# One step for both head parities in the attention scores of a network's last two layers

## The chip, the cores and the metric

The program runs on one core of one Trainium2 chip. The metric is the device time of one execution in microseconds (us); the median of three runs of the kernel before is 1946.26 us (1945.66 to 1946.44).

## The reference, cut to what matters

Four layers work on 256 tokens of 1024 channels, in float32: one with a recurrent mixer (HGRN2), one with latent attention, and two of a second block, each with feed-forward parts. The change touches only the two attentions in the mixer of the second block's two layers. Both have 8 heads of 64 channels:

```python
# stick-breaking attention
z = jnp.einsum('bhqd,bhkd->bhqk', qi, k).astype(jnp.float32) * scale
past = kpos[None, :] < qpos[:, None]
log_keep = jnp.where(past, jax.nn.log_sigmoid(-z), 0.0)
suffix = lax.cumsum(log_keep, axis=3, reverse=True) - log_keep
w = jnp.where(past, jnp.exp(jax.nn.log_sigmoid(z) + suffix), 0.0)
return jnp.einsum('bhqk,bhkd->bhqd', w.astype(v.dtype), v)
...
# block attention: with 256 tokens a query sees only its own block
s_own = jnp.einsum('bhqd,bhkd->bhqk', qi, k_own).astype(jnp.float32) * scale
s_own = jnp.where(own_pos[None, :] <= qpos[:, None], s_own, -jnp.inf)
p = jax.nn.softmax(jnp.concatenate([s_sel, s_own], axis=-1), axis=-1).astype(v.dtype)
```

## The kernel before

The tokens are two blocks of 128, called 0 and 1 here (`t` in the code); block 1 attends to the keys of both. Weights stream in chunks of 1024 columns per partition; each is split once, on ScalarE (high part, `wh`) and VectorE (low part, `wl`), and both token blocks use it. A projection multiplies the 128 tokens with a chunk by six products of 128x512 columns (three for each of two blocks of rows: L438, L439, L440, by `mm3`). Such a piece is called a chunk step below. Up to 11 split chunks are kept.

The program's work is cut into steps that begin with products on TensorE (`add`). They stand in lanes; a planner (`run`) picks the next step of all lanes by its own clock, from the costs that each step states, its dependences, the free PSUM banks and the free pages of two arenas (`fa` for float32, `ra` for float32r). So each engine's instructions have one fixed order, and a step whose costs change can move everything behind it. Where a step's turn comes, its ScalarE and VectorE instructions are queued there too, and the chunk splits take their places between them.

The mixer (`mixer`, one for each layer and token block) has, beside its projections, these steps:
- `turn` (L1441): four transposes that bring the queries or keys of four pairs of heads to [channel, token]. The two heads of a pair (even and odd parity) lie on rows 0 to 63 and 64 to 127. Queries and keys of the block attention are first rotated on GpSimd.
- `sb_z(g, kb)` (L1462, L1464): stick-breaking scores of the four heads of parity g against key block kb, into one bank: for the diagonal block a product of the identity with the mask (128x512), then four products with 64 rows. Then a chain of ScalarE (absolute value, exponential, logarithm, copy) and VectorE. `sb_suffix` (L1488 and following) and `sb_mix` (L1515) use it.
- `mb_s(i)` (L1547, L1551, L1552): scores of the block attention, 2 units for token block 0 with four heads each and 4 units for block 1 with two heads each, each of one parity in one bank. For every head a mask product of 128 columns and the head's product follow each other; for block 1 the products with the keys of block 0 come ahead. Then `softmax`: maximum on VectorE, exponentials on ScalarE, reciprocal and scaling on VectorE.
- `mb_t` (L1566): four transposes of a unit's weights, copied back by VectorE; `mb_o` (L1587): products with the values.

A float32 product of the program is two records in the trace.

Of the kernel before, what the change touches and what calls it, by code (L numbers as in the profile page):

```python
# [26 lines left out]
# Weights stream through the chip in chunks of at most 1024 columns per partition,  # L27
# loaded two (or so) at a time; each chunk is split once into float32r parts
# (high + low) that both token blocks use.
RAW = 3           # loads in flight  # L30
RING = 11         # split chunks kept
AHEAD = 2         # chunks split ahead of their first use
FAR = 5           # the same, while the engines that split have less than SLACK to do
SLACK = 0.9       # microseconds
LEAD = 6          # chunks token block 0 may be ahead of token block 1
DVE_LEVELS = 3    # levels of HGRN2 whose queries are decayed by the vector engine
SPARE = 3328      # words that a projection of HGRN2 leaves to the heads at work
HOP = 0.4         # from one engine to another, microseconds
ARENA_F = 9728    # float32 words per partition
ARENA_R = 6144    # float32r words per partition  # L40
# [3 lines left out]
class Arena:  # L44
    def __init__(self, tile_, words):
        self.t = tile_
        self.n = words // PAGE
        self.free_at = [0] * self.n     # 0: never used; None: held
        self.clock = 1

    def fits(self, words, spare=0):
        """Room for this many words in all, in pieces of up to 1024."""
        k = (words + PAGE - 1) // PAGE
        if sum(f is not None for f in self.free_at) < k + spare // PAGE:
            return False
        size, want = min(k, 8), max(k // 8, 1)
        run = found = 0
        for f in self.free_at:
            run = 0 if f is None else run + 1
            if run and run == size:  # L60
                found, run = found + 1, 0
        return k == 0 or found >= want
# [29 lines left out]
class Step:  # L92
    """Work that begins with products: its time on the tensor engine, the steps and the chunk that it
    waits for, the PSUM banks that it takes and gives back, and the words (float32, float32r, float32
    to be left free) without which it isn't begun."""
# [14 lines left out]
def constants():  # L110
    """Tables that depend on shapes alone."""
    i = np.arange(P)
    ident = np.eye(P)
    causal = np.where(i[None, :] > i[:, None], NEG, 0.0)       # [query, key]
    strict = np.where(i[:, None] >= i[None, :], NEG, 0.0)      # [key, query]
    after = (i[:, None] > i[None, :]).astype(float)            # [key', key]
    ones = np.ones((P, P))
    parts = {"ident": ident, "causal": causal, "strict": strict, "after": after, "ones": ones}
    # decay exponents of HGRN2: for a level of half-length m the pair (s, t) meets at
    # the middle of the 2m-block that splits them  # L120
# [29 lines left out]
def network_kernel(ctx: ExitStack, tc: tile.TileContext, A, out):  # L150
    nc = tc.nc
    mm = nc.tensor.matmul
    # the clock by which steps are ordered: when each engine is free, and how far the
    # work behind the step at hand has come
# [8 lines left out]
    def mark():  # L163
        """The banks of the step are read."""
        chain[2] = chain[0]

    class Engine:
        """An engine whose instructions are charged by the columns they write."""
# [24 lines left out]
    def act(o, i, func, with_ln=False, **k):  # L193
        """An activation; with_ln: natural logarithms come with it."""
# [36 lines left out]
    rope1 = sb.tile([P, 2, 2, 32], F32, name="rope1")      # [token, block, cos|sin, :]  # L231
    rope2 = sb.tile([P, 2, 2, 8], F32, name="rope2")
    krT = sb.tile([P, 2, 2 * P], F32, name="krT")     # rows of the other head of a pair are zero
# [20 lines left out]
    chunks, loads = [], []  # L254

    def load(dmas, views):
        """dmas: (columns of the raw buffer as a function, source); views: chunks cut from it."""
# [11 lines left out]
    def load_cols(w, k0, c0, n):  # L269
        """Four blocks of rows, n columns of each: two chunks of 2 x n."""  # L270
# [4 lines left out]
    def load_pair(w, c0, wc, n):  # L275
        """Two blocks of rows, wc columns: chunks of 2 x n."""
# [4 lines left out]
    def load_rows(w, k0):  # L281
        """Two whole blocks of rows: two chunks of 1 x 1024."""
# [4 lines left out]
    def load_gu(wg, wu, j, half):  # L287
        """Columns of gate and up side by side."""
        v = lambda r: r.rearrange("p (k g f) -> p k g f", k=4, g=2)
        dmas = []  # L290
        size = 4 if loads else 2     # the first chunk is waited for
# [20 lines left out]
    def with_gain(chs, g):  # L312
        """The rows of the chunks, which follow each other, are scaled by the gains from column g of gcol."""
# [29 lines left out]
    def splits(now, upto, slack=None):  # L343
        """Split chunks up to the given one; with a slack, only while the engines are idle enough."""
# [16 lines left out]
    def add(t, key, pe, emit, deps=(), chunk=None, banks=(), acq=(), rel=(), lane="", need=(0, 0)):  # L361
        """Steps of one lane run in order; the main lane of a token block is called ""."""
# [4 lines left out]
    def ready(s):  # L367
        if not fa.fits(s.need[0], *s.need[2:]) or not ra.fits(s.need[1]):
            return None
# [78 lines left out]
    def project(t, key, chs, xh, xl, evac, deps=(), n=512, behind=None, need=512, spare=0):  # L448
        """out[tokens, n] over the blocks of rows of chs, evacuated by evac(psum); behind: adds steps
        that follow the first chunk."""  # L450
# [21 lines left out]
    def down(t, key, chs, lhs, deps, first, evac=None, end=None):  # L472
        """Blocks of rows of a product with 1024 columns, summed in two banks: the first half of the
        columns of all, then the second. The last step has an evac(bank, half)."""
# [16 lines left out]
    def downs(t, key, chs, lhs, deps, evac, end=None):  # L491
        """The blocks one by one, but the last two together."""
# [5 lines left out]
    def transposes(t, key, g, deps):  # L498
        """X -> X^T in parts (XH, XL), scaled by the gains from column g of gcol per row, if given."""
# [25 lines left out]
    def split_scaled(src, g, h, l):  # L525
        """Parts of src * g, one gain per partition and block, src in PSUM."""
# [18 lines left out]
    pending = [None, None]     # statistics, put behind the first chunk that follows  # L545

    def norm_tr(t, key, g, xdep):
        """RMS statistics of X and its transposed parts scaled by the gain g."""
# [104 lines left out]
    def ple(t, li, W, g, xdep):  # L653
# [31 lines left out]
        for n in (0, 1):  # L685
            def evac(o, n=n):
                s = F(512)
                c = slice(n * 512, n * 512 + 512)
                # sigmoid(y) = (1 + tanh(y / 2)) / 2, the last half in pw
# [25 lines left out]
    def hgrn_tables(t):  # L715
        """Bounds of the forget gates, decay exponents and masks."""
        for hf in (0, 1):
            hg["lb", hf] = F(D)     # the bound, and 1 - the bound
# [43 lines left out]
    def hgrn(t, W, g, xdep):  # L762
# [12 lines left out]
        def evac(hf, c):  # L775
            def f(o):
# [24 lines left out]
                else:  # L801
                    s = F(512)
                    # sigmoid(y) = (1 + tanh(y / 2)) / 2
# [20 lines left out]
        def diagonal(hf):  # L824
            """A token's own key: sum of q * k."""
# [12 lines left out]
        def suffix(hf):  # L838
            """Keys decayed to the end of the block, token-major."""
# [30 lines left out]
        def stepA(hd):  # L870
            """Keys and queries decayed to the middle of the blocks of every level."""
# [45 lines left out]
        def stepB(hd):  # L917
            """Scores as [key, query]: what the halves of a block of 32 and more give goes straight
            to its place, the four small levels are computed for their later tokens and masked."""
# [112 lines left out]
    kvs = {}  # L1032

    def rope1_table(t):
        """cos and sin of position * inverse frequency, reduced to [-pi, pi]."""
# [829 lines left out]
```

## Time and profile before

| | |
|---|---|
| runs | 1945.66, 1946.26, 1946.44 us |
| profiled execution, span | 1944.4 us |
| TensorE matmul busy | 1915.5 us (99%) |
| VectorE, ScalarE, GpSimd busy | 1208.8 us (62%), 1026.6 us (53%), 181.5 us (9%) |
| first and last start of L1464 | 1187.5 and 1596.4 us |
| first and last start of L1552 | 1245.6 and 1656.5 us |

The span is the profiled execution's own, from its first to its last instruction; its time as a run was not recorded, and the span is 1.9 us below the median of the runs. TensorE is busy nearly all the time, in the two mixers (near 1170 to 1290 us and 1535 to 1660 us) too, so its queue is what to read first; an idle time of another engine costs nothing by itself.

### The profile page before, as it was taken

To read this page: it belongs to the slowest core of one execution; us is meant where nothing else is said; L and a number is where in the kernel's file an instruction comes from. 1 tells how busy PE (TensorE), PEld (TensorE's weight loads), DVE (VectorE), ACT (ScalarE), POOL (GpSimd) and SP (SyncE) were. 2 spreads that over 40 slices of the span, in tenths; PEclk is the share of its full clock that TensorE was granted. 3 is DMA by queue.
4 is the path that set the end of the run, shared out by engine and by line. 5 is a ranking of instruction groups with operands and counts; after the bars stand their busy time and mean duration, and the time that the engine had idled before them with its cause. 6 is when DMAs were issued, how large, how long until landed. Compare 5 with 4: busy or idle time off the path is not lost. (4 is left out here: it accounts for less than half of the span.)

```text
span 1944.4 us, 25096 instructions
## 1 busy us (share of the span) xinstructions
PE 1915.5 (99%) x9484; PEld 1586.2 (82%) x9484; DVE 1208.8 (62%) x1804; ACT 1026.6 (53%) x1596; POOL 181.5 (9%) x320
## 2 busy tenths in 40 slices
PE   8999989999999999999999999999999999999998
PEld 6888878888888888899888888778888887888886
DVE  6567769855567555556655566666655665666554
ACT  6565655644457555665544456544544465544442
POOL 1021334200001000232000000200000002000000
PEclk9999999999999999999999999999999999999999
DMA  9656313666546655333666653345656534556661
GB/s 289 223 183 192 117 60 107 195 196 200 182 149 194 208 183 189 109 114 132 194 194 187 201 173 131 124 165 189 206 184 214 175 109 131 176 192 196 193 215 45
DMA packets 215509, 331.30 MB, mean 170 GB/s; under 512 B 8462, under 2 KB 150236, under 8 KB 215388
## 3 DMA queue, kind: packets, MB, share of 16 engines
q1 hardware_dynamic: 215020, 329.14, 52.3%
q8 instruction: 74, 1.21, 0.3%
q10 hardware_dynamic: 368, 0.56, 0.1%
q14 instruction: 47, 0.39, 0.1%
HBM read 328.62 MB, written 1.05 MB: 170 GB/s over the span
## 5 line engine op out<-in xcount | busy, mean ns | idle before, releaser
L181 DVE TENSOR_TENSOR wl<-raw,wh 128x1024 fp32r<-128x1024 f32 (+1 forms) x520 | 631.7, 1229 | 424.7 <-ACT wh L204 423.6
L204 ACT ACTIVATE wh<-raw 128x1024 fp32r<-128x1024 f32 (+1 forms) x520 | 538.3, 1050 | 345.2 <-PE bank L440 312.9
L438 PE MATMUL bank<-wh,xh 128*128 128x512 f32 x1696 | 682.2, 402 | 2.5 <-ACT wh L204 2.5
L440 PE MATMUL bank<-wh,xl 128*128 128x512 f32 x1696 | 664.6, 392 | 0.0
L439 PE MATMUL bank<-wl,xh 128*128 128x512 f32 x1696 | 663.6, 391 | 1.0 <-DVE wl L181 1.0
L440 PEld LDWEIGHTS bank<-wh,xl 128*128 128x128 f32 x1696 | 320.1, 189 | 68.7 <-DVE xl L181 0.8
L438 PEld LDWEIGHTS bank<-wh,xh 128*128 128x128 f32 x1696 | 320.6, 189 | 65.1 <-ACT wh L204 3.3
L439 PEld LDWEIGHTS bank<-wl,xh 128*128 128x128 f32 x1696 | 321.1, 189 | 62.9 <-DVE wl L181 3.3
L438 PE MATMUL bank<-wh,ra 128*128 128x512 f32 (+1 forms) x736 | 286.3, 389 | 0.5 <-ACT ra L204 0.5
L440 PE MATMUL bank<-wh,ra 128*128 128x512 f32 (+1 forms) x736 | 283.5, 385 | 0.1
L439 PE MATMUL bank<-wl,ra 128*128 128x512 f32 (+1 forms) x736 | 283.1, 385 | 0.0
L204 ACT ACTIVATE fa<-bank,stat 128x256 f32<-128x256 f32 (+4 forms) x198 | 95.8, 490 | 184.2 <-PE bank L440 132.8
L204 ACT ACTIVATE fa<-bank 128x512 f32<-128x512 f32 (+3 forms) x228 | 102.4, 480 | 141.7 <-PE bank L440 87.5
L440 PEld LDWEIGHTS bank<-wh,ra 128*128 128x128 f32 x736 | 138.1, 188 | 27.4 <-DVE ra L181 1.1
L438 PEld LDWEIGHTS bank<-wh,ra 128*128 128x128 f32 x736 | 138.4, 188 | 26.3 <-ACT ra L204 0.7
L439 PEld LDWEIGHTS bank<-wl,ra 128*128 128x128 f32 x736 | 138.3, 188 | 25.7
L181 DVE SCALAR_TENSOR_TENSOR wl<-raw,gcol,wh 128x512 fp32r<-128x512 f32 (+1 forms) x192 | 136.3, 759 | 35.5 <-ACT wh L204 33.6
L181 POOL TENSOR_TENSOR stat<-stat,mhalf 128x1 f32<-128x1 f32 (+1 forms) x34 | 28.1, 826 | 1306.3 <-DVE stat L181 1306.3
L204 ACT ACTIVATE wh<-raw,gcol 128x512 fp32r<-128x512 f32 (+1 forms) x192 | 126.2, 709 | 29.3 <-PE bank L440 21.1
L181 POOL TENSOR_TENSOR fa<-fa 128x64 f32<-128x64 f32 (+4 forms) x156 | 98.3, 654 | 178.5 <-DVE fa L181 102.0
L204 ACT ACTIVATE ra<-bank 128x256 fp32r<-128x256 f32 (+1 forms) x158 | 61.9, 391 | 83.4 <-PE bank L590 43.4
L181 DVE SCALAR_TENSOR_TENSOR fa<-bank,stat,fa 128x256 f32<-128x256 f32 x88 | 42.5, 483 | 84.6 <-ACT fa L204 84.6
(160 smaller groups left out, 1296.0 us busy)
## 6 DMA issues: line engine op xcount, KB each, us to landing
raw<-in_ffn_w_in_dram SPq DMA_DIRECT2D x174, 512.0 KB, 4.9
raw<-in_ffn_w_out_dram SPq DMA_DIRECT2D x44, 1024.0 KB, 4.9
raw<-in_w_in_dram SPq DMA_DIRECT2D x40, 1024.0 KB, 5.1
raw<-in_w_ffn_gate_dram SPq DMA_DIRECT2D x44, 512.0 KB, 4.0
raw<-in_w_ffn_up_dram SPq DMA_DIRECT2D x44, 512.0 KB, 5.0
raw<-in_w_ffn_down_dram SPq DMA_DIRECT2D x22, 1024.0 KB, 4.9
raw<-in_a_w_in_dram SPq DMA_DIRECT2D x16, 1024.0 KB, 5.4
raw<-in_ple_w_gate_dram SPq DMA_DIRECT2D x8, 1024.0 KB, 5.0
```

Source lines behind the costliest of these rows:

```text
L181: return f(o, *a, **k)
L204: nc.scalar.activation(o, i, func, **k)
L438: mm(o, xh, ch.h[:, kk, cols], start=start, stop=False)
L439: mm(o, xh, ch.l[:, kk, cols], start=False, stop=False)
L440: mm(o, xl, ch.h[:, kk, cols], start=False, stop=stop)
```

## The change

`sb_z` and `mb_s` now make both parities in one step, with two banks. The masks come first, one product per bank (identity times a 128x512 mask, or two heads' 128x256 in token block 1), then the heads' products, where even and odd parity, so rows 0 to 63 and 64 to 127 of the array, take turns, each into its own bank. In `sb_z` the three ScalarE instructions of both parities stand ahead of the VectorE part, and one buffer `sp` serves both parities in turn. `mb_t` writes the transposed weights back into its source. The steps' stated costs and arena needs change with it, and `fits` looks for the float32r room in pieces of 512 words.

```diff
@@ Arena.fits, ready @@
-    def fits(self, words, spare=0):
+    def fits(self, words, spare=0, piece=8):
...
-        size, want = min(k, 8), max(k // 8, 1)
+        size, want = min(k, piece), max(k // piece, 1)
...
-        if not fa.fits(s.need[0], *s.need[2:]) or not ra.fits(s.need[1]):
+        if not fa.fits(s.need[0], *s.need[2:]) or not ra.fits(s.need[1], 0, 4):
@@ mixer: stick-breaking scores @@
-        def sb_z(g, kb):
-            name = K(f"z{g}{kb}")
+        def sb_z(kb):
+            name = K(f"z{kb}")
+            banks = [f"{name}.{g}" for g in (0, 1)]
             def emit():
-                b = B(name)
+                bs = [B(n) for n in banks]
                 qT, kT = four(sh["qsT", t]), four(sh["ksT", kb])
-                r = slice(64 * g, 64 * g + 64)
                 if kb == t:
-                    mm(b, identb, strict.rearrange("p a b -> p (a b)"), start=True, stop=False)
+                    for b in bs:
+                        mm(b, identb, strict.rearrange("p a b -> p (a b)"), start=True, stop=False)
                 for i in range(4):
-                    mm(b[:, i * P:(i + 1) * P], kT[r, i], qT[r, i], start=kb != t, stop=kb != t or i == 3)
-                u, sp = F(512), F(512)
-                h, l = R(512), R(512)
-                act(u.ap, b, AF.Abs)
-                act(u.ap, u.ap, AF.Exp, with_ln=True, scale=-1.0)
-                act(u.ap, u.ap, AF.Ln, with_ln=True, bias=one)
-                stt(sp.ap, b, 0.0, u.ap, op0=OP.max, op1=OP.add)
-                act(h.ap, sp.ap, AF.Copy)
-                tt(u.ap, b, sp.ap, op=OP.subtract)
-                mark()
-                tt(l.ap, sp.ap, f32(h.ap), op=OP.subtract)
+                    for g, b in enumerate(bs):
+                        r = slice(64 * g, 64 * g + 64)
+                        mm(b[:, i * P:(i + 1) * P], kT[r, i], qT[r, i], start=kb != t, stop=kb != t or i == 3)
+                us = [F(512), F(512)]
+                sp = F(512)
+                for b, u in zip(bs, us):
+                    act(u.ap, b, AF.Abs)
+                    act(u.ap, u.ap, AF.Exp, with_ln=True, scale=-1.0)
+                    act(u.ap, u.ap, AF.Ln, with_ln=True, bias=one)
+                for g, (b, u) in enumerate(zip(bs, us)):
+                    h, l = R(512), R(512)
+                    stt(sp.ap, b, 0.0, u.ap, op0=OP.max, op1=OP.add)
+                    act(h.ap, sp.ap, AF.Copy)
+                    tt(u.ap, b, sp.ap, op=OP.subtract)
+                    if g:
+                        mark()
+                    tt(l.ap, sp.ap, f32(h.ap), op=OP.subtract)
+                    st["u", g, kb], st["sp", g, kb] = u, (h, l)
                 sp.free()
...
-            add(t, name, 0.86 + 0.22 * (kb == t), emit,
+            add(t, name, 0.9 + 0.44 * (kb == t), emit,
...
-                lane="z", need=(1024, 1024))
+                lane="z", need=(1536, 2048))
@@ mixer: block attention @@
-        def mb_s(i):
+        def mb_s(w):
...
-                if t == 1:
-                    kT = four(sh["kmT", 0])
-                    for j, pr in enumerate(prs):
-                        mm(b[:, j, :P], qT[r, pr], kT[r, pr], start=True, stop=True)
-                kT = four(sh["kmT", t])
-                for j, pr in enumerate(prs):
-                    o = b[:, j, t * P:]
-                    mm(o, identb, causal[:, 0], start=True, stop=False)
-                    mm(o, qT[r, pr], kT[r, pr], start=False, stop=True)
-                p = F(512)
-                softmax(b, nh, p.ap.rearrange("p (h s) -> p h s", h=nh))
+                for b in bs:
+                    mm(b[:, :, t * P:], identb, causal[:, :nh], start=True, stop=False)
+                for kb in range(nk):
+                    kT = four(sh["kmT", kb])
+                    for j, pr in enumerate(mb_pairs(w)):
+                        for hf, b in enumerate(bs):
+                            r = slice(64 * hf, 64 * hf + 64)
+                            mm(b[:, j, kb * P:(kb + 1) * P], qT[r, pr], kT[r, pr], start=False,
+                               stop=kb == nk - 1 and j == nh - 1)
+                for hf, b in enumerate(bs):
+                    p = st["P", 2 * w + hf] = F(512)
+                    softmax(b, nh, p.ap.rearrange("p (h s) -> p h s", h=nh))
...
-            add(t, name, 1.0, emit, deps=[K("tqm")] + [f"{kb}.{key}.tkm" for kb in range(nk)],
-                banks=[name], lane="s", need=(512, 0))
+            add(t, name, 1.2, emit, deps=[K("tqm")] + [f"{kb}.{key}.tkm" for kb in range(nk)],
+                banks=banks, lane="s", need=(1024, 0))
@@ mb_t: the transposed weights go back over p @@
-                p.free()
-                y = F(512)
-                vec.tensor_copy(y.ap, b)
-                st["PT", i] = y
+                vec.tensor_copy(p.ap, b)
+                st["PT", i] = p
```

The change moves instructions, on TensorE inside the steps and on all engines by the planner. On TensorE, the scores of token block 0 in the first mixer (`ident` is the identity, `strict` the mask, `fa` queries and keys); before:

```order
L1462 LDWEIGHTS identb
L1462 MATMUL bank_111<-strict,identb 128x512
L1464 MATMUL bank_111<-fa 128x128 x4
L1462 LDWEIGHTS identb
L1462 MATMUL bank_112<-strict,identb 128x512
L1464 MATMUL bank_112<-fa 128x128 x4
```

and now:

```order
L1465 LDWEIGHTS identb
L1465 MATMUL bank_111<-strict,identb 128x512
L1465 LDWEIGHTS identb
L1465 MATMUL bank_112<-strict,identb 128x512
L1469 MATMUL bank_111<-fa 128x128
L1469 MATMUL bank_112<-fa 128x128
L1469 MATMUL bank_111<-fa 128x128
L1469 MATMUL bank_112<-fa 128x128
L1469 MATMUL bank_111<-fa 128x128
L1469 MATMUL bank_112<-fa 128x128
L1469 MATMUL bank_111<-fa 128x128
L1469 MATMUL bank_112<-fa 128x128
```

The two masks stand together, and the products change bank, so row half, from one to the next.

On ScalarE, from the evacuation of the projected block attention keys of token block 0 (the first row) to the copy of their transposes (the last row); between them GpSimd rotates these keys. Before, with the transposed queries of block 1 and two splits (`wh`) between:

```order
L204 ACTIVATE fa<-bank_107 128x512
L204 ACTIVATE fa<-bank_109 128x512
L204 ACTIVATE wh_75<-raw_65 128x1024
L204 ACTIVATE wh_76<-raw_65 128x1024
L204 ACTIVATE fa<-bank_108 128x512
```

and now, where the keys of block 1 and the mix of block 1 (`ra`) are between as well:

```order
L204 ACTIVATE fa<-bank_107 128x512
L204 ACTIVATE fa<-bank_114 128x512
L204 ACTIVATE fa<-bank_113 128x512
L204 ACTIVATE wh_75<-raw_65 128x1024
L204 ACTIVATE ra<-bank_112 128x512
L204 ACTIVATE wh_76<-raw_65 128x1024
L204 ACTIVATE fa<-bank_110 128x512
```

On TensorE the transposes of these keys stood behind four transposes and two chunk steps; they now stand behind five chunk steps, four transposes and the 16 products of a mix.

On ScalarE, around the exponentials of block 1's four softmax units (rows with `fa,stat<-bank`); before, from the copy of block 0's output (`ra`):

```order
L204 ACTIVATE ra<-bank_112 128x512
L204 ACTIVATE fa,stat<-bank_111,stat 128x256 x2
L204 ACTIVATE fa,stat<-bank_113,stat 128x256 x2
L204 ACTIVATE fa,stat<-bank_107,stat 128x256 x2
L204 ACTIVATE fa,stat<-bank_108,stat 128x256 x2
L198 ACT_TABLE_LOAD
L204 ACTIVATE fa<-bank_110 128x512
```

and now, after the splits `wh_67` and `wh_68`:

```order
L204 ACTIVATE wh_67<-raw_63 128x1024
L204 ACTIVATE wh_68<-raw_64 128x1024
L204 ACTIVATE fa,stat<-bank_112,stat 128x256 x2
L204 ACTIVATE fa,stat<-bank_110,stat 128x256 x2
L204 ACTIVATE wh_69<-raw_64 128x1024
L204 ACTIVATE fa,stat<-bank_114,stat 128x256 x2
L204 ACTIVATE fa,stat<-bank_109,stat 128x256 x2
L204 ACTIVATE wh_70<-raw_65 128x1024
```

All four units were one run; now two of a step stand together, with a split between the steps, and the split `wh_70`, which the first chunk step of the next weight waits for, stands behind all four.

## Rows read from the trace of the kernel before

**Rows 1.** The page, part 1: busy us, share of the span, instructions.
```profile
PE 1915.5 (99%) x9484; PEld 1586.2 (82%) x9484; DVE 1208.8 (62%) x1804; ACT 1026.6 (53%) x1596; POOL 181.5 (9%) x320
```

**Rows 2.** Windows: busy us by engine (instructions), then granted clock, DMA share, GB/s.
```profile
1267.90:1274.80 6.90, 6.90 (x24) 5.21 (x25) 3.62 (x10) 2.91 (x12) 0.00 (x0) 0.51 0.12 46
1633.20:1640.00 6.80, 6.80 (x17) 5.11 (x18) 4.00 (x13) 4.38 (x16) 0.00 (x0) 0.50 0.00 0
```

**Rows 3.** Timeline of TensorE, first mixer, block 0's z steps: start, us, engine, line.
```profile
1187.14 0.39 PE L1462 MATMUL bank<-strict,identb 128*128 128x512 bf16 x1
1187.46 1.16 PE L1464 MATMUL bank<-fa 64*128 64x128 f32 x8
1188.54 0.39 PE L1462 MATMUL bank<-strict,identb 128*128 128x512 bf16 x1
...
1189.95 0.50 PE L438 MATMUL bank<-wh,xh 128*128 128x512 f32 x1
```

**Rows 4.** The same, block 1's z steps.
```profile
1208.07 0.39 PE L1462 MATMUL bank<-strict,identb 128*128 128x512 bf16 x1
1208.39 2.05 PE L1464 MATMUL bank<-fa 64*128 64x128 f32 x16
...
1212.67 0.50 PE L438 MATMUL bank<-wh,xh 128*128 128x512 f32 x1
```

**Rows 5.** The same, keys' transposes and block 0's softmax scores; [idle before, releaser].
```profile
1241.34 0.39 PE L439 MATMUL bank<-wl,xh 128*128 128x512 f32 x1
1241.56 0.39 PE L440 MATMUL bank<-wh,xl 128*128 128x512 f32 x1
1243.61 0.66 PE L1441 MATMUL bank<-ident,fa 128*128 128x128 f32 x4 [1.66 <-POOL fa L181]
...
1245.49 0.23 PE L1551 MATMUL bank<-causal,identb 128*128 128x128 bf16 x1
...
1250.10 0.50 PE L438 MATMUL bank<-wh,xh 128*128 128x512 f32 x1
```

**Rows 6.** The same, block 1's softmax scores.
```profile
1263.66 0.71 PE L1547 MATMUL bank<-fa 64*128 64x128 f32 x4
...
1265.04 0.37 PE L1552 MATMUL bank<-fa 64*128 64x128 f32 x1
1265.05 0.37 PE L1547 MATMUL bank<-fa 64*128 64x128 f32 x1
...
1270.76 0.79 PE L438 MATMUL bank<-wh,xh 128*128 128x512 f32 x1
```

**Rows 7.** The same, second mixer.
```profile
1627.61 0.66 PE L1441 MATMUL bank<-ident,fa 128*128 128x128 f32 x4 [1.66 <-POOL fa L181]
...
1629.49 0.23 PE L1551 MATMUL bank<-causal,identb 128*128 128x128 bf16 x1
...
1634.74 0.79 PE L438 MATMUL bank<-wh,xh 128*128 128x512 f32 x1
...
1650.75 0.71 PE L1547 MATMUL bank<-fa 64*128 64x128 f32 x4
...
1656.69 0.50 PE L438 MATMUL bank<-wh,xh 128*128 128x512 f32 x1
```

**Rows 8.** Timeline of VectorE, first mixer, softmax units, split and copy.
```profile
1247.90 0.69 DVE L181 TENSOR_REDUCE stat<-bank 128x4 f32<-128x512 f32 x1 [0.79 <-PE bank L1552]
...
1251.23 0.68 DVE L181 TENSOR_REDUCE stat<-bank 128x4 f32<-128x512 f32 x1
...
1254.64 1.22 DVE L181 TENSOR_TENSOR wl<-raw,wh 128x1024 fp32r<-128x1024 f32 x1
1255.78 0.68 DVE L181 COPY fa<-bank 128x512 f32<-128x512 f32 x1
...
1265.57 0.69 DVE L181 TENSOR_REDUCE stat<-bank 128x2 f32<-128x512 f32 x1 [0.47 <-PE bank L1552]
...
1268.07 0.68 DVE L181 TENSOR_REDUCE stat<-bank 128x2 f32<-128x512 f32 x1
```

More of the change, by code (lines that the diff above doesn't have):

```diff
@@ L1475, in emit @@
+                for g, (b, u) in enumerate(zip(bs, us)):
[7 more added lines that the diff above has]
+                    st["u", g, kb], st["sp", g, kb] = u, (h, l)
                 sp.free()
-                st["u", g, kb], st["sp", g, kb] = u, (h, l)
@@ L1477, in sb_z @@
-            add(t, name, 0.86 + 0.22 * (kb == t), emit,
-                deps=[K("tqs"), f"{kb}.{key}.tks"], banks=[name],
-                lane="z", need=(1024, 1024))
+            add(t, name, 0.9 + 0.44 * (kb == t), emit,
+                deps=[K("tqs"), f"{kb}.{key}.tks"], banks=banks,
+                lane="z", need=(1536, 2048))
         def sb_suffix(g, kb):
@@ L1501, in emit @@
                 act(u.ap, u.ap, AF.Exp)
-            add(t, name, 0.43 if kb == t else 0.86, emit, deps=[K(f"z{g}{t}"), K(f"z{g}{kb}")],
+            add(t, name, 0.43 if kb == t else 0.86, emit, deps=[K(f"z{t}"), K(f"z{kb}")],
                 banks=[name], lane="y")
@@ L1530, in mixer, with mb_pairs @@
         nh = 4 if t == 0 else 2
-        def mb_heads(i):
-            return [nh * (i // 2) + j for j in range(nh)], i % 2
-        def mb_s(i):
-            name = K(f"s{i}")
+        def mb_pairs(w):
+            return [nh * w + j for j in range(nh)]
+        def mb_s(w):
+            name = K(f"s{w}")
+            banks = [f"{name}.{hf}" for hf in (0, 1)]
             def emit():
-                b = B(name).rearrange("p (h s) -> p h s", h=nh)
+                bs = [B(n).rearrange("p (h s) -> p h s", h=nh) for n in banks]
                 qT = four(sh["qmT", t])
-                prs, hf = mb_heads(i)
-                r = slice(64 * hf, 64 * hf + 64)
-                if t == 1:
-                    kT = four(sh["kmT", 0])
-                    for j, pr in enumerate(prs):
-                        mm(b[:, j, :P], qT[r, pr], kT[r, pr], start=True, stop=True)
-                kT = four(sh["kmT", t])
-                for j, pr in enumerate(prs):
-                    o = b[:, j, t * P:]
-                    mm(o, identb, causal[:, 0], start=True, stop=False)
-                    mm(o, qT[r, pr], kT[r, pr], start=False, stop=True)
-                p = F(512)
-                softmax(b, nh, p.ap.rearrange("p (h s) -> p h s", h=nh))
-                st["P", i] = p
-            add(t, name, 1.0, emit, deps=[K("tqm")] + [f"{kb}.{key}.tkm" for kb in range(nk)],
-                banks=[name], lane="s", need=(512, 0))
+                for b in bs:
[12 more added lines that the diff above has]
+                banks=banks, lane="s", need=(1024, 0))
         def mb_t(i):
@@ L1566, in emit @@
                     nc.tensor.transpose(b[:, j * P:(j + 1) * P], p.ap[:, j * P:(j + 1) * P], ident)
-                p.free()
-                y = F(512)
-                vec.tensor_copy(y.ap, b)
-                st["PT", i] = y
-            add(t, name, 0.44, emit, deps=[K(f"s{i}")], banks=[name],
-                lane="x", need=(512, 0))
+                vec.tensor_copy(p.ap, b)
+                st["PT", i] = p
+            add(t, name, 0.44, emit, deps=[K(f"s{i // 2}")], banks=[name], lane="x")
         def mb_o(w):
@@ L1579, in emit @@
                 ys = [st.pop(("PT", 2 * w + hf)) for hf in (0, 1)]
-                prs, _ = mb_heads(2 * w)
-                for j, pr in enumerate(prs):
+                for j, pr in enumerate(mb_pairs(w)):
                     for hf in (0, 1):
@@ L1606, in mixer @@
             turn(n)
+        for kb in reversed(range(nk)):
+            sb_z(kb)
         for g in (0, 1):
-            for kb in reversed(range(nk)):
-                sb_z(g, kb)
             for kb in reversed(range(nk)):
@@ L1614, in mixer @@
             turn(n)
-        for i in range(2 * nk):
-            mb_s(i)
-            mb_t(i)
-            if i % 2:
-                mb_o(i // 2)
+        for w in range(nk):
+            mb_s(w)
+            mb_t(2 * w)
+            mb_t(2 * w + 1)
+            mb_o(w)
         def proj(n, chs, evac, **k):
```

## Prediction

> **What bounds the kernel now.** The page's shares come first: TensorE has products in hand 99% of the span, the next engine 62% [rows 1]. So the time is what TensorE's queue takes, and the timeline of TensorE is the next view, at the score steps that change. It shows three costs. First, the scores themselves, which I measure from a step's first product to the first product behind it. In the first mixer these are 2.81 us [rows 3], 4.60 us [rows 4], 4.61 us (1245.49 to 1250.10) [rows 5] and 7.09 us [rows 6]. In the second the softmax scores take 5.25 and 5.94 us [rows 7], and I take its z steps as in the first, 7.41 us. Together 19.1 and 18.6, so 37.7 us. Second, the clock: for 6.9 us in the first mixer and 6.8 us in the second the windows show a granted clock of 0.51 and 0.50, the 1.2 GHz level [rows 2]. Both stretches begin inside softmax score steps, after 4.2 us of them (from 1263.66) and 3.7 us (from 1629.49), and run on over plain chunk steps. Third, a wait: the keys' transposes start 2.05 us after the product ahead of them, where 0.22 us is usual, released by GpSimd [rows 5]; the second mixer has the same idle time of 1.66 us [rows 7].
>
> **The price of a score step.** A float32 product is two records. Eight records of one row half take 1.08 us up to the next mask, sixteen show 2.05 against 1.16 us [rows 3, 4]: (2.05 - 1.16) / 8 = 0.111 us each, and 1.08 - 6 x 0.111 = 0.41 us for getting in and out of the 64-row form. A 512-column mask stands 0.32 us ahead of the first record [rows 3], a second such mask would add what a 512-column product takes, 0.22 us [rows 5].
>
> **What halves by turns cost.** The kernel before has this at one place: where a unit of one parity ends and one of the other begins, the first records of both start at 1265.04 and 1265.05, in different halves and banks [rows 6]. So I take two halves to run side by side, and 2 x n records to take 0.41 + (n - 2) x 0.111 us. The bounds: nothing shared (0.41 + (2n - 2) x 0.111, a rival below) and this; I take this, since the row shows the very pairing. The Trainium skill, "TensorE: Matmul & The Clock Gate", section "Measured speedup vs the span model", gives 3.07 for four row tiles instead of 4; if two fell short as much, a spacing would be 0.145 us (an estimate from that page), which over the 76 spacings of the sum would take 2.6 us from the gain. No run shown so far has a longer stretch of turns that could decide.
>
> **The scores after, for each mixer.**
> - Block 0's z step: 0.22 + 0.32 + 0.41 + 6 x 0.111 = 1.62 us.
> - Block 1's two z steps, one behind the other, eight products per half: 0.54 + 0.41 + 14 x 0.111 = 2.50 us.
> - Block 0's softmax scores: 1.62 us.
> - Block 1's two softmax steps: masks of 256 columns, no row, between 0 and the 0.54 us of the wide pair; I take 0.32, as they are half as wide and keep the change of form. 0.32 + 0.41 + 0.67 = 1.40 us, twice 2.80 us (the bounds are 1.3 us lower and 0.9 us higher for both mixers).
> Sum 8.5 us, two mixers 17.1 us: **-20.6 us** on TensorE's queue.
>
> **The clock.** With steps of 1.4 to 2.5 us, apart, in place of runs of 5 to 7 us I expect no fall there. What it cost inside the scores is in the 20.6. Outside, half of 1270.76 to 1274.8 and of 1634.74 to 1640.0 comes back: 2.0 + 2.6 = **-4.6 us**. Before, runs of 4.6 us [rows 4, 5] and one of 5.9 us [rows 7] kept the high clock, so a fall is not certain even for long runs.
>
> **The keys' wait.** The planner puts five chunk steps (1.35 us each), four transposes and the mix between the projected keys and their transposes, where before there were two chunk steps and four transposes. That covers both the rotation and the two later places that the evacuation now has on ScalarE. 2 x (2.05 - 0.22) = **-3.6 us**. If the cover fails it stays, at most.
>
> **What is late next: the softmax units.** They are unchanged in work: 3.33 us for a unit of block 0 (1247.90 to 1251.23), 2.50 for one of block 1 (1265.57 to 1268.07), a split's low part 1.14, a copy 0.6 [rows 8]. VectorE's order now has, from the end of block 0's scores: two units 6.7, split, copy, split, copy 3.5 (after waiting about 0.3 for ScalarE), two units 5.0, two copies and a split 2.3, two units 5.0, then the split that belongs to `wh_70`, with ScalarE's part ahead of it 1.5: 24.3 us. TensorE comes to that chunk after two score steps of 1.4, twelve chunk steps of 1.35 (six products of 0.22 to 0.23), seven sets of four transposes at 0.4 (four records), and one product with the values, eight records a half, of 1.1: 2.8 + 16.2 + 2.8 + 1.1 = 22.9 us. The difference is a wait of 1.4 us for each mixer, at the last unit's transposes or at this split; the bounds are 0 and, with VectorE's chain a tenth longer, 3.8. I take 1.4, which the rows give: **+2.8 us**. For the z steps I count no wait: the first step that needs their result stands seven chunk steps behind, where there were two. SP and GpSimd have the same instructions in the same order.
>
> **Sum.** -20.6 - 4.6 - 3.6 + 2.8 = -26.0 us against the profiled span of 1944.4: 1918.4. The median of the runs is 1.9 us above that span, so I forecast **1920 us**; with the bounds of masks, wait and softmax 1916 to 1926.
>
> **Rivals.**
> 1. The clock falls again, in one mixer or both. For it: the softmax steps, transposes and value products of block 1 still follow each other closely, and VectorE's waits come at the same place. Against it: each run is shorter than any after which it fell. A stretch as in [rows 2] costs half of 6.8, 3.4 us: 1923 to 1927 us.
> 2. Evacuation binds. The scores come out of TensorE sooner, but the softmax units still take 2 x 3.33 + 4 x 2.50 us on VectorE and ScalarE, in order with the splits. If that chain sets the pace, what the softmax steps save is waited for again: at the high clock 4.61 + 5.94 - 4.42 = 6.1 us for each mixer in place of the 1.4. That leaves 26.0 - 2 x 4.7 = 16.6 us: 1930 us. For it: the chain comes out longer than TensorE's work above already. Against it: for that loss the chain would have to be a fifth longer than its rows. The Trainium skill, "TensorEngine Tiling (Array Packing)", section "PSUM Bottleneck", warns of just this, that tiling speeds TensorE but not the evacuation; the near tie is as far as the trace bears it out.
> 3. The change doesn't do what it says: halves do not share. Then a mixer's scores take 2.50 + 4.28 + 2.50 + 2 x 2.28 = 13.9 us, 27.7 in both, and 10.7 us of the gain go: 1931 us, and up to 1936 if the longer runs let the clock fall as before. Against it: the two records 10 ns apart [rows 6].
> 4. The other side, slower: turning from half to half costs what a change of form costs. Every record then pays about 0.2 us of getting in and out besides its 0.111. With 192 records and 2.2 us of masks per mixer that is 64 us of scores in place of 37.7; with the keys' wait gone and the clock as before 1969 us. It decides from (37.7 + 3.6 - 4.4) / 192 = 0.19 us a record. Against it again [rows 6].
>
> **How the numbers follow.** Forecast 60%, rival 1 15%, rival 2 12%, rival 3 6%, rival 4 3%, and 4% for something else around no change. 0.2% is 3.9 us, about what a measurement of this kernel can tell from no change. The forecast and the first three rivals are all faster by more, 93%, and with 1 of the last 4 it is 94%; within it 2%; slower 4%. The range of 1914 to 1931 holds the forecast, rival 1 and nearly all of rival 2, and 2 us below the forecast's own range for costs that I set too high.
>
> **What would show it.** Right: in the timeline the odd and even records of a score step start in pairs some 0.11 us apart, block 0's steps end after 1.6 us and block 1's z steps after 2.5; the granted clock of the mixers is 1.00; the keys' transposes have no idle time ahead of them; about 1 us of idle time ahead of the weights' transposes or a chunk step that waits for `wl`. Wrong: pairs 0.22 us apart (rival 3), idle times of several us behind the softmax (rival 2), a window at 0.5 (rival 1), records over 0.19 us apart (rival 4).

## The result, and the profile after

| | before | after |
|---|---|---|
| median of the runs | 1946.35 us | 1921.34 us (1919.53 to 1922.41, 4 runs) |
| ratio to before | | 0.9868, interval 0.9852 to 0.9884 |
| profiled execution, span | 1944.4 us | 1920.6 us (its time 1922.41 us) |
| first transposes of the first mixer | 1175.78 us | 1179.24 us |

The change is 25.0 us faster by the medians; 1920 was forecast. The page's part 1 after, against [rows 1]:

```profile
PE 1892.9 (99%) x9458; PEld 1569.5 (82%) x9464; DVE 1206.8 (63%) x1804; ACT 1025.0 (53%) x1596; POOL 175.5 (9%) x320
```

TensorE is still busy 99% of the span, so what it has less to do is what the change is worth. The last line of the table needs care. Ahead of the first mixer both kernels have the same products, yet the changed one reached it 3.5 us later. The windows (columns as in [rows 2]) put the mixers side by side, each from its first transposes of queries to the layer norm's transposes behind it, first before, then after:

```profile
1175.78:1360.76 184.98, 183.32 (x934) 148.28 (x933) 117.62 (x150) 100.14 (x153) 13.58 (x25) 0.98 0.47 159
1559.78:1744.82 185.04, 183.38 (x934) 148.25 (x933) 117.22 (x150) 100.26 (x153) 12.26 (x25) 0.98 0.46 154
```
```profile
1179.24:1350.54 171.30, 170.78 (x920) 139.14 (x922) 116.08 (x150) 99.27 (x153) 10.41 (x25) 1.00 0.50 171
1549.55:1721.01 171.46, 170.76 (x920) 139.14 (x922) 116.05 (x150) 99.26 (x153) 10.41 (x25) 1.00 0.49 166
```

The mixers fell from 370.0 to 342.8 us, by 27.2 us, and all of their time after has the full granted clock. VectorE's and ScalarE's busy time in them hardly changed. The part between the mixers (199.0 us) and the part behind the second (199.6 us) are the same in both profiles. So the change gave 27.2 us where it was made, and the profiled executions differ by 3.5 us, the other way, in a part that it doesn't touch; the spans differ by the rest, 23.8 us.

TensorE's timeline after, at the places of [rows 3, 4, 5 and 6] (one of the two masks of L1465 and L1553 is missing from the records in the first three):

```profile
1190.83 0.38 PE L1465 MATMUL bank<-strict,identb 128*128 128x512 bf16 x1
1191.14 1.16 PE L1469 MATMUL bank<-fa 64*128 64x128 f32 x16
1192.23 0.50 PE L438 MATMUL bank<-wh,xh 128*128 128x512 f32 x1
...
1213.30 0.38 PE L1465 MATMUL bank<-strict,identb 128*128 128x512 bf16 x1
1213.61 2.06 PE L1469 MATMUL bank<-fa 64*128 64x128 f32 x32
1215.59 0.50 PE L438 MATMUL bank<-wh,xh 128*128 128x512 f32 x1
...
1245.83 0.39 PE L440 MATMUL bank<-wh,xl 128*128 128x512 f32 x1
1246.06 0.60 PE L1441 MATMUL bank<-ident,fa 128*128 128x128 f32 x4
...
1248.12 0.38 PE L1553 MATMUL bank<-causal,identb 128*128 128x512 bf16 x1
1248.43 1.16 PE L1559 MATMUL bank<-fa 64*128 64x128 f32 x16
1249.52 0.66 PE L1441 MATMUL bank<-ident,fa 128*128 128x128 f32 x4
...
1260.59 0.39 PE L1553 MATMUL bank<-causal,identb 128*128 128x256 bf16 x2
1260.92 1.16 PE L1559 MATMUL bank<-fa 64*128 64x128 f32 x16
1262.01 0.50 PE L438 MATMUL bank<-wh,xh 128*128 128x512 f32 x1
```

Sixteen score records now take the 1.16 us that eight of one half took [rows 3]. The keys' transposes at 1246.06 follow the product ahead of them by 0.23 us, and the 1.66 us of idle time [rows 5] are gone. The one new wait comes later, at a chunk step whose product with `wl` waits for VectorE's split, in both mixers:

```profile
1273.23 0.47 PE L438 MATMUL bank<-wh,ra 128*128 128x512 f32 x1
1274.03 0.50 PE L439 MATMUL bank<-wl,ra 128*128 128x512 f32 x1 [0.32 <-DVE wl L181]
...
1643.53 0.47 PE L438 MATMUL bank<-wh,ra 128*128 128x512 f32 x1
1644.50 0.50 PE L439 MATMUL bank<-wl,ra 128*128 128x512 f32 x1 [0.49 <-DVE wl L181]
```

### The profile page after: what moved, and what is told of

Read it like the earlier page. It is cut to its first block, busy times and chain, and to the rows that moved or that the text cites. A ratio compares the mean times of both kernels' runs of the same rounds, so it can differ in the third digit from the quotient of the medians.

```text
span 1920.6 us, 25043 instructions
## 1 busy us (share of the span) xinstructions
PE 1892.9 (99%) x9458; PEld 1569.5 (82%) x9464; DVE 1206.8 (63%) x1804; ACT 1025.0 (53%) x1596; POOL 175.5 (9%) x320
```

## The experiments

My theory is the prediction's: the two halves run side by side, the masks' merging saves changes of form, and the planner's new order takes the keys' wait away. The rivals are that turns are worth nothing and the merged masks everything, or that the new order of steps gives most of it. "Scores" below are all score steps of both mixers from a step's first record to the next other product, as in the prediction; where a first mask is not recorded, 0.23 us (0.32 with products of a half behind it) are put in for it. "Mixers" are the two stretches of the windows above, added, in the one profiled execution of each kernel; they tell kernels apart better than the medians, which carry the spread of the part ahead. A "fall" is a stretch at half clock.

| kernel | scores | mixers | at half clock in them | median | ratio, interval |
|---|---|---|---|---|---|
| before | 37.7 | 370.0 | 13.7 | 1946.35 | |
| after | 17.2 | 342.8 | 0 | 1921.34 | 0.9868 (0.9852 to 0.9884) |
| after, once more | 17.2 | 342.9 | 0 | 1921.12 | 0.9868 (0.9850 to 0.9885) |
| grouped only | 35.5 | 361.7 | 3.4 | 1939.48 | 0.9962 (0.9947 to 0.9977) |
| no turns | 23.1 | 347.4 | 0 | 1922.97 | 0.9880 (0.9866 to 0.9895) |
| turns, masks apart | 21.1 | 345.7 | 0 | 1925.05 | 0.9887 (0.9872 to 0.9902) |
| turns in twos | 18.2 | 343.2 | 0 | 1919.57 | 0.9860 (0.9843 to 0.9876) |
| z steps only | | 353.9 | 0 | 1932.07 | 0.9934 (0.9918 to 0.9951) |
| softmax steps only | | 350.5 | 0 | 1927.34 | 0.9906 (0.9891 to 0.9921) |
| keys later | | 362.2 | 3.4 | 1942.13 | 0.9979 (0.9969 to 0.9988) |
| softmax more | 17.2 | 347.2 | 3.4 | 1921.42 | 0.9867 (0.9851 to 0.9884) |
| block 1's copies on ScalarE | 17.2 | 343.4 | 0 | 1919.68 | 0.9861 (0.9845 to 0.9877) |
| block 0's copies on ScalarE | 17.2 | 342.8 | 0 | 1918.90 | 0.9855 (0.9830 to 0.9881) |

**No turns.** In the changed kernel, the loop over the halves outside:

```diff
-                for i in range(4):
-                    for g, b in enumerate(bs):
-                        r = slice(64 * g, 64 * g + 64)
+                for g, b in enumerate(bs):
+                    r = slice(64 * g, 64 * g + 64)
+                    for i in range(4):
```

and so in `mb_s`. Expected:

> The changed kernel with both masks first, but all products of one row half and then all of the other; order of the steps as in the changed kernel. Theory (two halves run side by side on TensorE): a step of 2 x n records goes back to 0.41 + (2n - 2) x 0.111 us: block 0's z and softmax steps 2.50 us, block 1's two z steps 4.28, its softmax steps 2.28 each, 13.8 us a mixer where the changed kernel has 8.6. That is +10.5 us in both mixers, of which the 0.3 and 0.5 us of waiting behind the softmax are taken back: 1931 us; 1934 to 1938 if the clock falls again beside the longer steps. Rival (the gain is the merged masks and the new order of steps, turns are worth nothing): 1921 to 1922 us, steps of 1.6 us.

Measured: the mixers took 347.4 us, 4.6 more than with turns, the scores 5.9 more. Neither the theory nor the rival had this. Turns are worth something in the mixers, so the rival falls; the medians, 1922.97 and 1921.34 us, would hardly have shown it. But a step without turns takes less than I reckoned. Its timeline, and then windows of its L1469 alone (length, then products and weight loads with the number of each in flight):

```profile
1186.57 0.38 PE L1465 MATMUL bank<-strict,identb 128*128 128x512 bf16 x1
1186.88 1.71 PE L1469 MATMUL bank<-fa 64*128 64x128 f32 x16
1188.52 0.50 PE L438 MATMUL bank<-wh,xh 128*128 128x512 f32 x1
```
```profile
1187.20:1187.31 0.11, 0.11 (x3) 0.11 (x2) 1.00 2.57 130
...
1187.77:1187.86 0.09, 0.09 (x6) 0.09 (x3) 1.00 1.49 137
...
1187.98:1188.09 0.11, 0.11 (x4) 0.11 (x2) 1.00 0.38 93
```

The sixteen records take 1.64 us; 0.41 + 14 x 0.111 would be 1.96. In the middle of the step twice as many products are in flight as ahead of it. Record by record, the second half's first (the only other one of 0.373 us in the step) starts at 1187.432 us, 6 ns behind the fifth of the first half's eight, and the first half's last, which signals its bank, at 1187.761. So three records of the second half have started before the first half is through, and the hand-over saves three spacings, 0.33 us. There are seven such hand-overs in a mixer of this kernel, 4.6 us in both mixers. That is the gap between the expected 27.7 and the measured 23.1 us of scores.

**Turns in twos.** The changed kernel with groups of two products, as `for i0 in (0, 2)`, then the halves, then `for i in (i0, i0 + 1)`. Expected:

> The changed kernel with the halves by turns in groups of two products (four records) in place of one. In the run without turns the second half's first record starts with the fifth of the first half's eight, so TensorE begins a half four records before its place in the queue. Theory (that look ahead is all that sharing needs, so groups of four records share fully): block 0's z step 1.40 us from its second mask to the next chunk step as with turns, block 1's two 2.3 us, both mixers together 342.8 us from the first transposes to the transposes behind them. Rival (only strict turns share fully): between 1.40 and the 1.95 us of the run without turns, mixers 344 to 346 us.

```profile
1187.90 0.60 PE L1465 MATMUL bank<-strict,identb 128*128 128x512 bf16 x2
1188.44 1.26 PE L1470 MATMUL bank<-fa 64*128 64x128 f32 x16
1189.63 0.50 PE L438 MATMUL bank<-wh,xh 128*128 128x512 f32 x1
```

Measured: 1.19 us from the first score record to the chunk step, where strict turns take 1.09 and no turns 1.64: one spacing more. Seven pairs stand side by side from the first records on, and two records alone, one in the middle and one at the end. The step's 1.50 us from its second mask lies just above the theory's 1.40, so by the letter in the rival's range; the mixers' 343.2 us lie below the rival's 344. The theory holds but for that spacing: TensorE finds the other half's records a few places further back by itself. The scores are 1.0 us longer in both mixers, of which 0.6 come out of waits, and the medians cannot tell the two apart.

**Grouped only.** The changed kernel's steps with the products of the kernel before inside. Expected:

> The changed kernel's steps and their order, but inside a step the products stand as in the kernel before: one half after the other, in the z steps each bank's mask ahead of its products, in the softmax steps a mask of 128 columns ahead of each head's product. Theory: the scores cost what they did, 35.9 us for both mixers at the high clock, so 18.7 us more than in the changed kernel; the keys' wait stays away: 1939 us if the clock holds, 1943 to 1946 if it falls in the softmax steps as before. The clock is the point here: before, it fell after 3.7 and 4.2 us of closely following softmax steps, and these are now apart (block 1's four units in two pairs). Rival (the new order of the steps gives most of the gain): under 1932 us.

Measured: 1939.48 us, as the theory with the clock held gave. One fall is left. It begins at the end of block 0's softmax scores, which run from 1248.57 to 1253.29 us:

```profile
1253.00:1256.40 3.40, 3.40 (x12) 2.70 (x12) 1.65 (x6) 1.51 (x9) 0.00 (x0) 0.50 0.00 0
```

What a fall costs can be counted product by product. Within one, chunk products of the kernel before stand 0.43 us apart, where 0.23 us is usual:

```profile
1635.76 0.63 PE L440 MATMUL bank<-wh,xl 128*128 128x512 f32 x1
1636.19 0.63 PE L438 MATMUL bank<-wh,xh 128*128 128x512 f32 x1
```

Against the same products at the full clock, the falls cost 6.2 us in before's mixers and 1.6 us in this kernel's. Without them before has 363.9 us of mixers and this kernel 360.1: the new order alone is worth 3.8 us, not most of the gain.

**Turns, masks apart.** In `mb_s` of the changed kernel, per pair of heads, the two masks and then the two products:

```diff
+                for j, pr in enumerate(mb_pairs(w)):
+                    for b in bs:
+                        mm(b[:, j, t * P:], identb, causal[:, 0], start=True, stop=False)
+                    for hf, b in enumerate(bs):
...
```

Expected:

> The changed kernel with turns, but in the softmax steps the masks stand apart: for each pair of heads two masks of 128 columns and then the pair's products by turns. Theory (each way in and out of the 64-row form costs some 0.4 us, whichever half): block 0's step has four such ways in place of one, 4 x 0.64 = 2.6 us in place of 1.6, block 1's steps 0.63 + 2 x 0.64 = 1.9 us in place of 1.4. That is 3.9 us in both mixers, less the 0.8 us of waits: 1924.5 us. Rival (merged masks are worth as much with turns as they are without, 8 us): 1929 us. Rival (they are worth nothing): 1921 us.

Measured: 1925.05 us, the mixers 2.9 us longer, the scores 3.9 us. One pair in block 0's step:

```profile
1247.36 0.29 PE L1561 MATMUL bank<-causal,identb 128*128 128x128 bf16 x2
1247.58 0.49 PE L1564 MATMUL bank<-fa 64*128 64x128 f32 x4
1248.00 0.29 PE L1561 MATMUL bank<-causal,identb 128*128 128x128 bf16 x2
```

0.64 us a pair, as the theory put it. Both rivals fall. The four kernels together show that the two parts don't add. Only the softmax steps can be compared so, as the z steps have their masks apart in grouped only alone. At the full clock the softmax steps of both mixers take 21.9 us with neither part, 12.8 with turns, 12.2 with merged masks and 8.9 with both. So turns save 9.1 us with masks apart and 3.3 with merged ones; merging saves 9.7 without turns and 3.9 with them. With masks apart, turns bring two heads into one way in and out of the 64-row form, 0.64 us in place of twice 0.58; with merged masks there is one such way a step in any case, and no mask keeps TensorE from overlapping the halves by itself.

**The two halves of the change.** The z steps as changed with the softmax steps of the kernel before, and the other way round. Expected:

> Only the stick-breaking part (the z steps) changed, block attention's softmax steps one per parity as in the kernel before. The planner then puts the mix and three chunk steps between block 1's queries' and keys' transposes, so the keys' wait should be gone. Theory: z steps 2 x (7.41 - 4.12) = -6.6 us, keys' wait -3.6 us: 1936 us with the clock falling in the softmax steps as before; if it does not fall, 1930 us.

> Only block attention's softmax steps changed, the z steps one per parity as in the kernel before; between the queries' and the keys' transposes of block 0 the order is that of the kernel before (two chunk steps). Theory: softmax scores 22.9 us (with the clock as it was) to 8.9 us, -14.0; clock outside the scores -4.6; the keys' wait of 1.8 us a mixer stays; a wait behind the softmax of about 0.4 us a mixer: 1928.5 us. Rival (the keys' wait goes with the softmax steps, not with the z steps): 1925 us. Together with the other half the gains should add up to that of the whole change.

Measured: 1932.07 us with the z steps alone, whose four runs (1929.1, 1930.1, 1934.0, 1935.6) lie about the theory's two values, with mean granted clocks of 0.996 in the first two and 0.994 in the others, and 1927.34 us with the softmax steps alone, near the theory's 1928.5. The z steps alone take the keys' wait away; in the timeline with the softmax steps alone it is all there:

```profile
1243.21 0.66 PE L1441 MATMUL bank<-ident,fa 128*128 128x128 f32 x4 [1.66 <-POOL fa L181]
```

Against 363.9 us at the full clock the mixers lose 9.9 and 13.4 us, together 23.3; the whole change takes 21.1. The new wait, which neither half alone has, is 1.1 of the 2.2 us between them; the rest was not traced.

**Keys later.** The kernel before, where the planner is told `chain[0] += 2.0` behind the keys' rotation. Expected:

> The kernel before, but the planner takes the rotated keys for ready 2.0 us later, so that four chunk steps in place of two stand ahead of block 0's keys' transposes; scores as before. Theory (GpSimd's rotation was late and nothing else): the wait of 1.8 us a mixer goes, -3.6 us: 1942.7 us. Rival (what is waited for there is waited for later, behind the softmax units, which start later by those steps): 1946 us.

Measured: 1942.13 us, ratio 0.9979 (0.9969 to 0.9988). The keys' transposes start with no idle time ahead of them:

```profile
1246.92 0.39 PE L440 MATMUL bank<-wh,xl 128*128 128x512 f32 x1
1247.15 0.60 PE L1443 MATMUL bank<-ident,fa 128*128 128x128 f32 x4
```

Of the 7.8 us that the mixers lost, 4.6 are smaller falls, so 3.3 are left for the wait of 3.7 us from start to start. TensorE's idle time in the mixers went from 3.3 to 0.6 us, none of it behind the softmax. So the wait was GpSimd's lateness, and two more chunk steps ahead of the transposes remove it.

**Softmax more.** In the changed kernel, `nc.vector.tensor_scalar(p.ap[:, c], p.ap[:, c], 1.0, None, op0=OP.mult)` for two halves `c` behind each softmax unit of block 1. Expected:

> The changed kernel with two more VectorE multiplications by 1.0 (256 columns each, 0.53 us together by the rows of the ones there) in each of block 1's four softmax units; order of steps unchanged. It asks how much room the softmax chain has left beside TensorE, which waits 0.3 and 0.5 us behind it. Theory (the chain and TensorE's work are as good as equal there, so that all that is added is waited for): 4 x 0.53 = 2.1 us a mixer, 1925.5 us, idle time of TensorE of some 2.5 us in each mixer. Rival (the waits shown are those of one late split alone and the chain has room ahead of it): 1921.5 us, idle time under 1 us.

```profile
1272.61 0.63 PE L1577 MATMUL bank<-ident,fa 128*128 128x128 f32 x4 [1.15 <-DVE fa L1566]
1272.99 0.47 PE L438 MATMUL bank<-wh,ra 128*128 128x512 f32 x1
1273.85 0.50 PE L439 MATMUL bank<-wl,ra 128*128 128x512 f32 x1 [0.39 <-DVE wl L181]
```

The two products, and the instruction behind them on VectorE:

```profile
1261.12 0.49 DVE L1566 TENSOR_SCALAR fa<-fa 128x256 f32<-128x256 f32 x2
1261.52 0.68 DVE L181 TENSOR_REDUCE stat<-bank 128x2 f32<-128x512 f32 x1
```

Measured: the theory, with a smaller addition. The two products took 0.40 us from start to start, not 0.53, so 1.6 us were added in a mixer. From the first unit to the end of the split the chain is 1.4 us longer (25.76 us for 24.35), and 1.4 us came out as time in the first mixer (172.7 us for 171.3), as idle time ahead of the last unit's transposes; the second has a fall besides. The chain has no more than 0.2 us of room. The median, 1921.42 us, doesn't show it; 2.8 us are less than the part ahead of the mixers varies.

**The copies.** Two tries at the wait that is left: `copy(p.ap, b)` in `mb_t` in place of `vec.tensor_copy`, first for block 1, then for block 0. Expected:

> The changed kernel with block 1's transposed weights copied out of PSUM by ScalarE in place of VectorE, four copies of 0.6 us a mixer. Theory (the 0.5 and 0.7 us of idle time left in each mixer are VectorE's chain of softmax units, copies and splits): idle time about 0.1 us, mixers 342.0 us in place of 342.8; the median of the runs can't tell this from the changed kernel. Rival (ScalarE, which must give the splits' high parts and the exponentials there, is as full): idle time 0.5 us or more, 343 us or more.

> The changed kernel with block 0's two transposed weights copied out of PSUM by ScalarE in place of VectorE; the run before this moved block 1's four copies, which stand on VectorE behind the split that TensorE waits for. These two stand ahead of block 1's last two softmax units and of that split. Theory (the idle time left in each mixer is VectorE's order of copies, units and splits): VectorE comes to that split 1.2 us earlier, the idle time of 0.3 and 0.5 us ahead of the chunk step that waits for wl goes, mixers 342.0 to 342.3 us. Rival (the units wait for ScalarE's exponentials, so that copies moved to ScalarE delay them as much): the same idle time, 342.8 us.

Measured: the idle time stays in both, 0.35 and 0.53, then 0.36 and 0.55 us; the mixers are 0.6 us longer in the first and the same in the second. In the first the copies stood behind the split in question, so it could not tell. In the second the 1.2 us that VectorE had less to do became idle time ahead of an earlier split, whose high part ScalarE now gave later:

```profile
1261.96 0.62 DVE L181 TENSOR_SCALAR fa<-fa,stat 128x256 f32<-128x256 f32 x2
1263.68 1.23 DVE L181 TENSOR_TENSOR wl<-raw,wh 128x1024 fp32r<-128x1024 f32 x1 [1.10 <-ACT wh L204]
```

What TensorE waits for is a chain that goes to and fro between the two engines, so moving these copies from one to the other was worth nothing there.

**The changed kernel once more.** Expected:

> The changed kernel once more, beside the two others on one chip. So far the stretch ahead of the first mixer, where all nine kernels have the same products, took 1174.6 to 1179.2 us, with 10 to 14 us of it at half clock. Theory (that part of the time differs from execution to execution and is no effect of the change): mixers 342.8 us again within 0.2, the start of the first mixer anywhere from 1174.6 to 1179.2 us, 1918 to 1923 us. Rival (the change delays that part): start again at 1179 us, with 13.6 us at half clock.

Measured: mixers 342.9 us, the first transposes at 1176.9 us, 10.2 us at half clock ahead of the mixers (13.7 in the first profile). The rival falls: those 3.5 us are no effect of the change. None of these kernels is faster than the changed one by more than the intervals.

## Why the prediction was right

- **The scores.** 37.7 to 17.1 us was forecast, 17.2 measured. Where all masks are recorded, in the second run of the changed kernel, the steps take 1.63 (z, block 0), 2.52 (z, block 1), 1.63 (softmax, block 0) and twice 1.41 us; forecast were 1.62, 2.50, 1.62 and 1.40. The 256-column masks that I had no row for cost the 0.32 us taken.
- **Halves side by side.** Fourteen of a step's sixteen records come as pairs 0.112 us apart behind the first pair, so nothing is lost beside one half alone. The Trainium skill, "TensorE: Matmul & The Clock Gate", section "Measured speedup vs the span model", has 3.07 for four row tiles, from which the prediction estimated 0.145 us for two; for two halves the trace does not agree, and no run here has four. Rivals 3 and 4 are out.
- **The clock.** No fall in the mixers in the profile of the changed kernel, either time: rival 1 did not come. In the profile of before two falls of 6.8 us cost 6.2 us, product by product: 4.4 outside the scores, where 4.6 was forecast, and 1.8 inside. But falls are not certain on either side. The 34 executions of before that were timed beside the variants have mean granted clocks of 0.991 to 0.996; the two shortest, 1943.39 and 1943.52 us at 0.995 and 0.996, are still some 22 us longer than the changed kernel's median, at 0.996. In the variants, z steps only kept the softmax steps of 4.6 us and shows none, and softmax more, with steps of 1.4 us, shows 3.4 us at half clock from 1645.90, behind 1.33 and 0.38 us of idle time. Short steps do not rule a fall out.
- **The keys' wait.** The order that the planner made removed it, by 2 x 1.83 us from start to start, and keys later showed it by itself.
- **The softmax wait** is the term that was mis-sized: 2 x 1.4 us were forecast, and the pairs of rows above give 0.80 and 0.97 us from the product with `wh` to that with `wl`, where 0.32 is usual behind transposes: 1.1 us. VectorE's chain was right, 24.3 us forecast and 24.35 measured from the first unit to the end of the split in the first mixer:

```profile
1249.62 0.69 DVE L181 TENSOR_REDUCE stat<-bank 128x4 f32<-128x512 f32 x1
...
1272.75 1.22 DVE L181 TENSOR_TENSOR wl<-raw,wh 128x1024 fp32r<-128x1024 f32 x1
```

TensorE's 22.9 us were too few. The twelve chunk steps took 16.8 us, not 16.2, as a step behind transposes or scores starts with one product of 0.31 to 0.34 us; the transposes took 3.0 for 2.8; and the product with `wh` ahead of the waiting one doesn't wait. So 24.0 us stood against 24.35 and some 0.1 us from engine to engine. Rival 2 (evacuation binds) did not come at its 4.7 us a mixer, but a small part of it did: the chain ends 0.5 us too late in the first mixer, and softmax more shows that what is added to it is paid nearly in full.
- **The sum.** With the measured terms the mixers lose 20.5 + 4.4 + 3.7 - 1.1 = 27.5 us; they lost 27.2. The forecast's 26.0 was short by the wait, 1.7 us. That the medians differ by 25.0 is partly luck: in the profiled executions the part ahead of the mixers was 3.5 us slower in the changed kernel, and its share in the other runs was not seen. So the forecast of 1920 is nearer to the median than its terms deserve.

## What to carry to other kernels

Price small products by their spacing and their changes of form, and look first for what stands between them: here a mask between the two halves cost its own change of form and the overlap as well. Of the 21.1 us that the mixers lost at the full clock, the new order of steps is 3.8, merged masks without turns 12.7 more, and strict turns the last 4.6. Where a kernel has a part whose time varies from execution to execution, compare the stretch that a change touches between the same two products, not the spans. Ahead of counting a wait, count the work of the engine that would wait to the product that waits, with its dearer first product behind every change of form.

## What was not expected of the hardware

- TensorE started products of the second row half ahead of products of the first that stand before them in its queue: the second half's first record 6 ns behind the fifth of eight. The Trainium skill, "TensorE: Matmul & The Clock Gate", section "The mechanism", has products start strictly in their order; by the records of the run without turns that does not hold between row halves. The kernel before shows it too. At [rows 6] L1547's first record, of the next unit, starts ahead of L1552's second, which stands before it in the queue:

```profile
1265.26 0.27 PE L1552 MATMUL bank<-fa 64*128 64x128 f32 x1
```

I took that pair for what strict turns would do; it is two halves one behind the other, overlapping by themselves.
- The part ahead of the first mixer, with the same products in every kernel, took 1174.6 to 1179.2 us in the thirteen profiles, with 6.8 to 13.7 us at half clock. The half clock is not all of it: turns in twos came to the mixer at 1176.5 us with 6.8 us of it, z steps only at 1174.6 with 10.2. What sets it was not tried.
